# Up product's whole tiles in one 512-wide piece, turns reordered, and late forms of the down product queued behind streamed weights

## The chip, the cores and the metric

The kernel runs on one core of one Trainium2 chip. The metric is the device time of one execution in microseconds (us); less is better. Three runs of the kernel before gave 828.09, 829.57 and 830.15 us, so the median is 829.57 us.

## The reference, cut to what matters

One layer of an encoder trunk, on 512 positions (`SEQ`) of width 1024. The change touches only the second half, a gated MLP with a convolution of width 3 between the two products, and the norm that leads into it:

```python
x = x + _rmsnorm(merged @ w_out, g_post_mix)
h2 = _rmsnorm(x, g_pre_ffn)
x = x + _rmsnorm(_conv_gated_mlp(h2, w_up, conv_w, conv_b, w_down), g_post_ffn)
...
hid = h @ w_up                        # 1024 -> 2 * 2816
hid = conv(hid, width 3) + conv_b     # along the positions, each column by itself
a, b = jnp.split(hid, 2, axis=-1)
return (jax.nn.gelu(a) * b) @ w_down  # 2816 -> 1024
```

All is float32.

## The kernel before, in words

**Numbers as pairs.** Each float32 operand of a large product is split into a high part, rounded to TensorE's `float32r` format, and a low part, the rest (`split`, line 85: ScalarE copies the high part at line 80, VectorE subtracts at line 87, so most of VectorE's work has line 87). A product then takes three matmuls: high by high, high by low, low by high (`mm3`, lines 219 to 221). In a matmul one operand of 128 columns is loaded into the array (LDWEIGHTS, the engine PEld of the profile) and the other streams past it, 256 or 512 columns wide.

**The weights** come in 146 blocks of 128 x 1024 from one tensor `wall`, each by one DMA on SyncE's queue, into 4 raw buffers. They are split into 9 slots (`slot`, tag `w4`). `w_get` hands out the next block and lets the following ones be prepared ahead, as far as slots are free. A second pool, `blk`, holds 76 tiles of 128 x 512 for nearly everything else.

**Products of seven.** Many products are made in Strassen's manner, with seven smaller products in place of eight, from sums and differences of operands that ScalarE and VectorE (and GpSimd for some weights) prepare. In the up product these are `Pair`s (line 676); in the down product `products` (line 1062).

**From the mixing half to the MLP.** `dn_.finish(t, n)` ends the product with `w_out` for the 128 positions of tile `t` (0 to 3) and one half `n` of the columns (lines 830 to 832). `norms(t)` scales the result, adds the residual and makes the normed, scaled rows `xn` (line 882). `turn(t)` transposes them on TensorE (line 895) and, for each of four pieces, copies the high part `h2h` on ScalarE, copies the plain value `h2r` on ScalarE and makes the low part `h2l` on VectorE (line 901). Both `h2h` and `h2l` are kept in two groups, positions 0 to 255 (`T0`) and 256 to 511 (`T1`). The up product of the first four column tiles starts with their `T0` half (`early(e, 0)`, e from 0 to 3), while tiles 2 and 3 are still being normed; `turn(2)` stands after `early(0, 0)` and `turn(3)` after `early(3, 0)`. Then come the four `T1` halves.

**The up product** makes 44 tiles of 128 columns, two for each of 22 steps `i`. Steps 0, 1 (the early ones), 2, 3, 20 and 21 take both tiles whole: `up_block` runs eight slices `k` of the weights against `T0`, 24 matmuls, and then again against `T1`. Steps 4 to 19 go in eight couples: of the four tiles of a couple two are a `Pair` (seven products of 12 matmuls each, 256 wide) and two are whole; the second whole tile has part 3 of the Pair, two products, between its two halves. `tile_done` then does convolution (lines 971, 974, 978), gelu (985) and the product of the halves, `gp` (987).

**The down product** has 2 x 9 column tiles in the manner of seven and 4 whole ones, and goes over the 1024 output columns in two halves. In each half nine pairs `j` are taken one after the other; a pair is 42 matmuls on two weight units, `q` (loaded as it is, 128 x 768) and `t` (sums of four quarters, lines 185 to 190, 128 x 1024). After pairs 3 and 5 of the first half stand 48 matmuls for whole tiles (line 1079). `down_forms(j)` prepares the activation side of pair `j`: five steps on 128 x 256 and three on 128 x 512 on VectorE (lines 87, 1000 to 1003) and four copies on ScalarE. `two_parts` splits one whole tile. `EAGER = 7` of the nine forms are made during the up product: four at steps 7, 11, 13 and 17, three at steps 19, 20 and 21. The other two are made at pairs 1 and 3 of the down product, and one whole tile is split at each of pairs 0 to 3.

**What sets the order.** The program is traced in the order of the code, and a scheduler then orders each engine's instructions by priority and by its own idea of when inputs are there. Each engine runs its instructions strictly in that order. `tc.issue_after(ins)` forces the instructions of a block that run on `ins`'s engine to stand behind `ins` there.

## Time and profile before

| | us |
|---|---|
| median of three runs | 829.57 |
| the profiled execution, its own time | 826.92 |
| span of the profiled execution, first to last instruction | 825.1 |
| TensorE matmul (PE) busy | 814.5 |
| TensorE weight load (PEld) busy | 756.6 |
| VectorE (DVE) busy | 658.5 |
| ScalarE (ACT) busy | 429.7 |
| GpSimd (POOL) busy | 104.2 |

The stages around the change, read from the timeline of PE: the product with `w_out` ends at 471.6 us of the span; the `T0` halves of the early tiles and the last two turns follow until 485.6; the `T1` halves and the whole tiles of steps 2 and 3, then the couples; steps 20 and 21 end at 703.9; the first half of the down product runs to about 764 us, the second half to 808; the rest is the last norm and the output.

In a row of the timeline stand the start in us, the time it covers, the engine, the line, what is written and read, how many instructions the row merges, and in brackets the idle time before it with what ended it. Since matmuls overlap, the pace of PE is read from the starts of its matmuls and not from their durations: a row's duration of 0.28 us goes with a start every 0.11 us. The ends of matmuls are modelled, so a wait between two matmuls shows as a late start and only its last part as idle time.

### The profile page before, as it was taken

Reading aid. Unit: us, or ns where it says so; the run is one execution under the profiler, and the core shown is the slowest. Engines: PE = TensorE matmul, PEld = TensorE weight load, DVE = VectorE, ACT = ScalarE, POOL = GpSimd, SP = SyncE. Lnnn points to the kernel's source line nnn. Section 1 sums busy time; section 2 is a strip of 40 time slices with the busy share of each in tenths; the row PEclk is TensorE's granted clock in tenths of the full one; section 3 lists DMA queues with packets and bytes.
Section 4 is the critical chain, followed back from the end, with each engine's and each line's share of the span. In section 5 each row is a group of like instructions: output and inputs, shape, how many; then the busy total and the mean of one; then the engine's idle time right before and its main releaser. Section 6 shows DMA issues by size and latency. Waiting matters only on the chain. (4 is left out here: it accounts for less than half of the span.)

```text
span 825.1 us, 14353 instructions
## 1 busy us (share of the span) xinstructions
PE 814.5 (99%) x5728; PEld 756.6 (92%) x5728; DVE 658.5 (80%) x1076; ACT 429.7 (52%) x733; POOL 104.2 (13%) x108
## 2 busy tenths in 40 slices
PE   9999999999999999999999999999999999999995
PEld 7888888888999999999988899999999999999995
DVE  7489897878898687767765579679899899997956
ACT  6636445536665444444444556456566566644532
POOL 0010000103221111132221201111111100000002
PEclk9999999999999999999999999999999999999999
DMA  8733222213233333233459111333333341243334
GB/s 284 256 116 102 77 77 77 77 52 94 74 105 127 103 103 101 80 101 102 123 173 355 64 54 50 104 102 103 103 103 103 102 155 52 77 141 104 114 129 128
DMA packets 29252, 93.84 MB, mean 114 GB/s; under 512 B 3392, under 2 KB 4032, under 8 KB 29184
## 3 DMA queue, kind: packets, MB, share of 16 engines
q1 hardware_dynamic: 26784, 86.58, 32.5%
q0 software_dynamic: 1968, 6.03, 2.4%
q8 instruction: 45, 0.74, 0.4%
q10 hardware_dynamic: 432, 0.30, 0.1%
q14 instruction: 23, 0.19, 0.1%
HBM read 88.19 MB, written 4.72 MB: 113 GB/s over the span
## 5 line engine op out<-in xcount | busy, mean ns | idle before, releaser
L87 DVE TENSOR_TENSOR wl<-raw,wh 128x1024 fp32r<-128x1024 f32 (+1 forms) x93 | 109.6, 1187 | 49.2 <-PE ps L676 26.5
L80 ACT ACTIVATE wf<-raw 128x512 fp32r<-128x512 f32 x140 | 85.0, 626 | 102.4 <-PE ps L220 42.7
L87 DVE TENSOR_TENSOR wf<-raw,wf 128x512 fp32r<-128x512 f32 x140 | 110.1, 801 | 26.1 <-ACT wf L80 25.4
L220 PE MATMUL ps<-h2l,wh 128*128 128x256 f32 x448 | 123.7, 277 | 0.2 <-DVE h2l L901 0.2
L219 PE MATMUL ps<-h2h,wh 128*128 128x256 f32 x448 | 123.3, 277 | 0.0
L221 PE MATMUL ps<-h2h,wl 128*128 128x256 f32 x448 | 123.3, 276 | 0.0
L676 PE MATMUL ps<-sh,wf 128*128 128x256 f32 x640 | 119.1, 277 | 0.1
L80 ACT ACTIVATE wh<-raw 128x1024 fp32r<-128x1024 f32 (+2 forms) x95 | 93.0, 989 | 35.5 <-DMA raw<-wall 14.0
L676 PEld LDWEIGHTS ps<-sh,wf 128*128 128x128 f32 x640 | 100.7, 188 | 0.8 <-DVE c L704 0.3
L676 PE MATMUL ps<-sl,wf 128*128 128x256 f32 x320 | 88.5, 277 | 0.0
L220 PEld LDWEIGHTS ps<-h2l,wh 128*128 128x128 f32 x448 | 84.0, 188 | 0.7 <-DVE h2l L901 0.7
L219 PEld LDWEIGHTS ps<-h2h,wh 128*128 128x128 f32 x448 | 83.8, 188 | 0.3 <-ACT h2h L80 0.3
L221 PEld LDWEIGHTS ps<-h2h,wl 128*128 128x128 f32 x448 | 83.9, 188 | 0.0
L481 PE MATMUL ps<-wh,xh 128*128 128x512 f32 x192 | 75.0, 391 | 0.0
L482 PE MATMUL ps<-wl,xh 128*128 128x512 f32 x192 | 74.9, 390 | 0.0
L483 PE MATMUL ps<-wh,xl 128*128 128x512 f32 x192 | 74.8, 390 | 0.0
L168 POOL TENSOR_TENSOR raw<-raw,raw 128x512 f32<-128x512 f32 x20 | 34.9, 1743 | 241.0 <-DVE raw L166 217.0
L1062 PE MATMUL ps<-dh,fl 128*128 128x256 f32 x216 | 61.0, 282 | 0.0
L1062 PE MATMUL ps<-dl,fh 128*128 128x256 f32 x216 | 60.3, 279 | 0.5 <-DVE dl L87 0.5
L1062 PE MATMUL ps<-dh,fh 128*128 128x256 f32 x216 | 60.6, 280 | 0.0
L676 PEld LDWEIGHTS ps<-sl,wf 128*128 128x128 f32 x320 | 60.1, 188 | 0.5 <-issue 0.2
L676 PE MATMUL ps<-xh,wf 128*128 128x256 f32 x288 | 53.6, 278 | 0.0
(309 smaller groups left out, 2035.0 us busy)
## 6 DMA issues: line engine op xcount, KB each, us to landing
raw<-wall SPq DMA_DIRECT2D x145, 512.0 KB, 3.6
x<-x SPq DMA_DIRECT2D x22, 256.0 KB, 5.7
xT<-xT SPq DMA_DIRECT2D x8, 256.0 KB, 5.3
x<-x POOLq DMA_DIRECT2D x8, 256.0 KB, 2.4
xT<-xT POOLq DMA_DIRECT2D x4, 256.0 KB, 4.3
out<-zs SPq DMA_DIRECT2D x3, 256.0 KB, 3.4
cs<-cs SPq DMA_DIRECT2D x2, 256.0 KB, 4.0
gpm<-gpost POOLq DMA_DIRECT2D x2, 256.0 KB, 3.7
```

The costliest lines, as they stand in the source:

```text
L80: nc.scalar.activation(out=o, in_=i, func=AF.Copy)
L87: nc.vector.tensor_sub(lo, src, as32(hi))
L168: nc.gpsimd.tensor_tensor(out=w_raw["T2"], in0=w_raw["T1"], in1=w_raw["B22"], op=ALU.add)
L219: nc.tensor.matmul(o, ah, bh, start=start, stop=False)
L220: nc.tensor.matmul(o, ah, bl, start=False, stop=False)
L221: nc.tensor.matmul(o, al, bh, start=False, stop=stop)
L481: nc.tensor.matmul(acc[t], xh[k][:, c], wh[:, f], start=k == 0, stop=False)
L482: nc.tensor.matmul(acc[t], xh[k][:, c], wl[:, f], start=False, stop=False)
L483: nc.tensor.matmul(acc[t], xl[k][:, c], wh[:, f], start=False, stop=k == KD - 1)
L676: nc.tensor.matmul(o, w_[:, c], a_, start=first and k == n == 0, stop=k == 3 and n == 2, skip_group_check=True,)
L1062: nc.tensor.matmul(o, a_[:, c], w_[:, f], start=j == t == i == 0, stop=j == DP - 1 and i == 2 and n not in (M2, M3, M4), skip_group_check= ...
```

## The change

1. **Tiles.** `h2h` and `h2l` are now four tiles each that hold two slices `k` of all 512 positions, in a new pool `two` (8 tiles of 128 x 1024) which they share with the parts of the first input, `xh` and `xl`, and later with parts of the down product. In return `blk` shrinks from 76 to 60 tiles.
2. **Up product.** `up_block` multiplies each slice `k` against all 512 positions at once: 24 matmuls 512 wide instead of 48 that are 256 wide. Part 3 of a Pair now stands after the fourth of the eight slices. The early tiles stay in two halves. The weights of the whole tiles lose their shift within a slot.
3. **Turns.** `turn` makes high and low parts first and the four plain copies at its end. The scaled rows of tile 2 are made behind the low parts of `turn(1)` on VectorE. `turn(3)` moves into the middle of `early(3, 0)`.
4. **Down product.** `EAGER` falls to 5. Forms 5 to 8 and the four splits of whole tiles come after pairs 0 to 5, each block of them behind the low part of the next pair's `t` weights on VectorE. The parts of the forms 7 and 8 and of the last two whole tiles lie in `two`.

The core of the diff:

```diff
-NBLK = 76
+NBLK = 60
-EAGER = 7
+EAGER = 5
+WIDE = 7
+    def two(dt=F32R, n="two"):
+        return sb.tile([P, 2 * S], dt, tag="two", bufs=8, name=nm(n))
...
     def turn(t, zs):
...
             for i in range(2):
...
                 copy(hi, pf)
-                copy(raw, pf)
-                v.tensor_sub(lo, pf, as32(hi))
+                low = v.tensor_sub(lo, pf, as32(hi))
+                raws.append((raw, pf))
+        for raw, pf in raws:
+            copy(raw, pf)
+        return low
...
     def up_block(between=None):
-        w, o = w_get(), ps()
-        h2_block(w, o, T0)
-        if between:
-            between()
-        h2_block(w, o, T1)
+        (wh, wl), o = w_get(), ps()
+        for k in range(KD):
+            if between and k == KD // 2:
+                between()
+            c = slice(k * P, (k + 1) * P)
+            mm3(o, wh[:, c], wl[:, c], *h2(k, slice(0, S)), k == 0, k == KD - 1)
         return o
...
     for t in range(NT):
         acc = [dn_.finish(t, 0)]
         if t > 1:
-            turn(t - 2, zs[t - 2])
+            low = turn(t - 2, zs[t - 2])
+        if t == 3:
+            with tc.issue_after(low.ins):
+                zs[2] = scaled(*xq)
         acc.append(dn_.finish(t, 1))
-        zs[t] = norms(t, acc)
+        xq = norms(t, acc)
+        if t != 2:
+            zs[t] = scaled(*xq)
     early(0, 0)
     turn(2, zs[2])
     for e in range(1, EARLY):
-        early(e, 0)
-    turn(3, zs[3])
+        early(e, 0, (lambda: turn(3, zs[3])) if e == EARLY - 1 else None)
...
-    late = list(range(EAGER, DP))
+    later = (("w", 0), ("w", 1), ("f", 5), ("w", 2), ("f", 6), ("w", 3), ("f", 7), ("f", 8))
     for j in range(DP):
-        if j < WHOLE:
-            whole.append(two_parts(gp[2 * DP + j]))
-        if j % 2 and late:
-            down_forms(late.pop(0))
         products(m, j, steps if j == DP - 1 else {})
+        if j + 1 < DP:
+            with tc.issue_after(w_low["t", DOWN0 + j + 1]):
+                for kind, i in {0: later[:1], 1: later[1:3], 2: later[3:4], 3: later[4:6], 4: later[6:7], 5: later[7:]}.get(j, ()):
+                    if kind == "w":
+                        whole.append(two_parts(gp[2 * DP + i], i > 1))
+                    else:
+                        down_forms(i)
```

What this moves on the engines, at three places. Names carry a number of the tile; in `a<-b,c` the tile `a` is written from `b` and `c`. First TensorE, in the second whole tile of the last couple, where part 3 of the Pair (`wf`, `sh`, `h2h` as its operands, line 676 before and 682 after) comes in; `ps_7476` and `ps_7004` are the tile's accumulator. Before:

```order
L220 MATMUL ps_7476<-h2l_4394,wh_7360 128x256
L221 MATMUL ps_7476<-h2h_4386,wl_7361 128x256
L219 MATMUL ps_7476<-h2h_4386,wh_7360 128x256
L220 MATMUL ps_7476<-h2l_4394,wh_7360 128x256
L221 MATMUL ps_7476<-h2h_4386,wl_7361 128x256
L676 MATMUL ps_7326<-h2h_4389,wf_7204 128x256
L676 MATMUL ps_7326<-h2l_4397,wf_7204 128x256
```

And now:

```order
L225 MATMUL ps_7004<-h2h_4376,wl_6913 128x512
L223 MATMUL ps_7004<-h2h_4376,wh_6912 128x512
L224 MATMUL ps_7004<-h2l_4380,wh_6912 128x512
L225 MATMUL ps_7004<-h2h_4376,wl_6913 128x512
L682 MATMUL ps_6878<-h2h_4377,wf_6780 128x256
L682 MATMUL ps_6878<-h2l_4381,wf_6780 128x256
```

Part 3 comes in at the same share of the tile, but the tile's own matmuls are half as many and twice as wide, so that PE passes from 512 wide to 256 wide and back here; there are three such passages in each couple.

Second VectorE between `norms(2)` and `norms(3)`. `xn` are the scaled rows of tile 2, `h2l` the low parts of `turn(1)`, `z` and `x` the norm of the tile. Before:

```order
L873 TENSOR_TENSOR x_844_4735<-x_844_4735,z_4755 128x512
L846 SCALAR_TENSOR_TENSOR qs_4761<-q_4747 128x1
L882 SCALAR_TENSOR_TENSOR xn_4765<-x_843_4734,qr_4762,gpr_4379 128x512
L882 SCALAR_TENSOR_TENSOR xn_4767<-x_844_4735,qr_4762,gpr_4380 128x512
L901 TENSOR_TENSOR h2l_4391<-ps_4787,h2h_4383 128x2x128
L901 TENSOR_TENSOR h2l_4393<-ps_4798,h2h_4385 128x2x128
L901 TENSOR_TENSOR h2l_4392<-ps_4787,h2h_4384 128x2x128
L901 TENSOR_TENSOR h2l_4394<-ps_4798,h2h_4386 128x2x128
```

And now:

```order
L879 TENSOR_TENSOR x_828_4719<-x_828_4719,z_4739 128x512
L909 TENSOR_TENSOR h2l_4379<-ps_4763,h2h_4375 128x2x128
L909 TENSOR_TENSOR h2l_4380<-ps_4763,h2h_4376 128x2x128
L909 TENSOR_TENSOR h2l_4381<-ps_4772,h2h_4377 128x2x128
L909 TENSOR_TENSOR h2l_4382<-ps_4772,h2h_4378 128x2x128
L852 SCALAR_TENSOR_TENSOR qs_4785<-q_4731 128x1
L891 SCALAR_TENSOR_TENSOR xn_4789<-x_827_4718,qr_4786,gpr_4371 128x512
L891 SCALAR_TENSOR_TENSOR xn_4791<-x_828_4719,qr_4786,gpr_4372 128x512
```

The four low parts moved ahead of the two scaled rows and of the small sum `qs` that these wait for.

Third VectorE in the down product, up to the low part of the `t` weights of pair 3 (`dl` with 128x1024; `dl` with 128x768 is that of a `q`). `fa`, `fs`, `fl` and `gp` at 128x256 are steps of a form. Before:

```order
L87 TENSOR_TENSOR fl_7956<-gp_7571,fh_7955 128x512
L87 TENSOR_TENSOR fa_7959<-gp_7033,fa_7959 128x256
L1000 TENSOR_TENSOR fs_7962<-gp_7033,gp_7044 128x256
L185 TENSOR_TENSOR raw_8117<-raw_8063 128x512
L1001 TENSOR_TENSOR fs_7962<-fs_7962,gp_7033 128x256
L87 TENSOR_TENSOR fl_7968<-gp_7044,fh_7967 128x512
L1002 TENSOR_TENSOR gp_7033<-gp_7033 128x256
L87 TENSOR_TENSOR fl_7972<-fs_7962,fh_7971 128x512
L1003 TENSOR_TENSOR gp_7033<-gp_7044,fs_7962 128x256
L87 TENSOR_TENSOR dl_8008<-raw_8003,dh_8007 128x1024
```

And now:

```order
L91 TENSOR_TENSOR dl_7288<-raw_7283,dh_7287 128x1024
L194 TENSOR_TENSOR raw_7347<-raw_7347,raw_7323 128x256
L91 TENSOR_TENSOR fl_7380<-gp_7075,fh_7379 128x512
L91 TENSOR_TENSOR dl_7326<-raw_7323,dh_7325 128x768
L91 TENSOR_TENSOR fa_7383<-gp_6173,fa_7383 128x256
L1021 TENSOR_TENSOR fs_7386<-gp_6173,gp_6184 128x256
L1022 TENSOR_TENSOR fs_7386<-fs_7386,gp_6173 128x256
L91 TENSOR_TENSOR fl_7392<-gp_6184,fh_7391 128x512
L91 TENSOR_TENSOR dl_7352<-raw_7347,dh_7351 128x1024
```

Before, nearly the whole of form 7 stands ahead of the low part of pair 3's `t`, and forms 5 and 6 are already made by then (further up); now form 5 is the first that has been begun there, four steps of it stand ahead, and forms 6, 7 and 8 follow in the same way behind the weights of later pairs.

More of the change, by code (lines that the diff above doesn't have):

```diff
@@ L192, in w_down @@
         hi, lo = slot("dh", 16, w), slot("dl", 48, w)
-        split(hi, lo, raw)
+        w_low[form, i] = split(hi, lo, raw).ins
         return hi, lo
@@ L243, in load_x @@
         nc.sync.dma_start(t, xT[k])
-        h_, l_ = blk(F32R, "xh"), blk(F32R, "xl")
+        if k % 2 == 0:
+            xp2.append((two(n="xh"), two(n="xl")))
+        h_, l_ = (a[:, k % 2 * S : (k % 2 + 1) * S] for a in xp2[-1])
         nc.scalar.activation(out=h_, in_=t, func=AF.Copy, scale=col(PRE + k))
@@ L853, in tile_block @@
     gpm, gpf = bcast(gpost, "gpm"), bcast(gpre, "gpr")
-    h2h, h2l, h2r = ([[blk(dt, n) for _ in range(4)] for _ in range(2)]
-                     for dt, n in ((F32R, "h2h"), (F32R, "h2l"), (F32, "h2r")))
+    h2h, h2l = ([two(n=n).rearrange("p (i s) -> p i s", i=2) for _ in range(4)] for n in ("h2h", "h2l"))
+    h2r = [[blk(n="h2r") for _ in range(4)] for _ in range(2)]
     x1 = [[dp_.tile([P, S], F32, tag=f"x1_{t}{n}", name=f"x1_{t}{n}") for n in range(2)] for t in range(NT)]
@@ L877, in norms, with scaled @@
                 nc.gpsimd.dma_start(out[t, :, 0:S], xt[0])
+        return xt, q
+    def scaled(xt, q):
         sc, _ = row_scale(q)
@@ L896, in turn @@
             for i in range(2):
-                hi, lo, raw = (h[g][2 * n + i].rearrange(two, i=2)[:, :, c] for h in (h2h, h2l, h2r))
-                pf = p[:, 2 * i * P : 2 * (i + 1) * P].rearrange(two, i=2)
+                hi, lo = (h[2 * n + i][:, :, t * P : (t + 1) * P] for h in (h2h, h2l))
+                raw = h2r[g][2 * n + i].rearrange("p (i n) -> p i n", i=2)[:, :, c]
+                pf = p[:, 2 * i * P : 2 * (i + 1) * P].rearrange("p (i n) -> p i n", i=2)
                 copy(hi, pf)
-                copy(raw, pf)
-                v.tensor_sub(lo, pf, as32(hi))
+                low = v.tensor_sub(lo, pf, as32(hi))
[3 more added lines that the diff above has]
+        return low
     def h2(k, t):
-        f = slice((k % 2) * 256, (k % 2 + 1) * 256)
-        g = t.start // 256
-        return h2h[g][k // 2][:, f], h2l[g][k // 2][:, f]
+        return tuple(h[k // 2][:, k % 2, t] for h in (h2h, h2l))
     h2forms = {n: [None] * 4 for n in ("S1", "S2", "S3", "S4")}
@@ L987, in gated, with two_parts @@
         v.tensor_mul(gp[-1], ca, cb)
-    def two_parts(t):
-        h_, l_ = blk(F32R, "fh"), blk(F32R, "fl")
+    def two_parts(t, wide=False):
+        if wide:
+            w = two(n="fw")
+            h_, l_ = w[:, :S], w[:, S:]
+        else:
+            h_, l_ = blk(F32R, "fh"), blk(F32R, "fl")
         split(h_, l_, t)
```

25 lines of the change are left out of this document (14 added, 11 removed).

## The prediction, on record before the changed kernel was run

> **What bounds the kernel now.** I read the page first: its busy row and the chain that ended last.
>
> ```profile
> PE 814.5 (99%) x5728; PEld 756.6 (92%) x5728; DVE 658.5 (80%) x1076; ACT 429.7 (52%) x733; POOL 104.2 (13%) x108
> ```
>
> TensorE (PE) is busy for 99% of the span, so the kernel is bounded by the pace of its matmuls and by the few waits between them. Then I read busy times in stretches of 25 us (columns: PE, PEld, DVE, ACT, POOL busy with counts, granted clock, DMA share, GB/s).
>
> ```profile
> 425.00:450.00 25.00, 25.00 (x112) 20.71 (x111) 15.79 (x21) 13.17 (x22) 5.66 (x9) 1.00 0.79 290
> 500.00:525.00 25.00, 25.00 (x223) 25.00 (x222) 23.68 (x36) 14.68 (x24) 2.59 (x2) 1.00 0.26 86
> 700.00:725.00 25.00, 24.52 (x210) 24.31 (x209) 25.00 (x44) 15.89 (x25) 0.00 (x0) 1.00 0.26 85
> ```
>
> In the first stretch PE runs matmuls 512 wide, in the second matmuls 256 wide, twice as many. The clock is full in all. In the third, where the up product ends and the down product begins, VectorE (DVE) has no free time at all and PE makes 13 matmuls fewer than in the second. The wait list of PE has few rows here:
>
> ```profile
> PE ps L1062 <- DVE dl L87: 0.5, 1, 0.5
> PE ps L220 <- DVE h2l L901: 0.2, 1, 0.2
> ```
>
> These are idle times by modelled ends; the true size of a wait is read below from the starts in the timeline.
>
> **Change 1: 512 wide instead of 256.** First and last rows of two long undisturbed runs, 48 and 162 matmuls apart (16 and 54 times three):
>
> ```profile
> 426.31 0.39 PE L830 MATMUL ps<-wh,mh 128*128 128x512 f32 x1
> ...
> 437.19 0.39 PE L830 MATMUL ps<-wh,mh 128*128 128x512 f32 x1
> ```
>
> ```profile
> 499.74 0.28 PE L219 MATMUL ps<-h2h,wh 128*128 128x256 f32 x1
> ...
> 518.10 0.28 PE L219 MATMUL ps<-h2h,wh 128*128 128x256 f32 x1
> ```
>
> 10.88 / 48 = 0.2267 us at 512 wide and 18.36 / 162 = 0.1133 us at 256 wide. Twice the second is the first: a wide matmul takes as long as the two that it replaces, and the weight load that is saved was hidden. The change makes 576 wide matmuls (24 whole tiles of 24) from 1152 narrow ones; 576 x (0.2267 - 2 x 0.1133) = 0.0 us, with 0.2 us either way for the last digit. The Trainium skill ("TensorE: Matmul & The Clock Gate", section "Back-to-back issue gap") gives N / 2.4 + 2.5 ns between starts, so a fixed 2.5 ns per matmul, and by it, as an estimate, the 576 saved matmuls would give 1.4 us; the rows leave no room for it.
>
> But PE now changes width within the couples. That already happens earlier in the kernel, where a block of 24 wide matmuls stands between narrow ones:
>
> ```profile
> 305.16 0.40 PE L219 MATMUL ps<-gh,wh 128*128 128x512 f32 x1
> ...
> 310.62 0.28 PE L676 MATMUL ps<-sh,wf 128*128 128x256 f32 x1
> ...
> 311.20 0.39 PE L676 MATMUL ps<-sh,wf 128*128 128x256 f32 x2
> ```
>
> The block takes 5.46 us where 24 x 0.2267 are 5.44, and the next five, 310.62 to 311.20, take 0.58 where 5 x 0.1133 are 0.57: some 0.03 us a passage. There are three in each of 8 couples and one at steps 2 and 3: 25 x 0.03 = 0.8 us more, on PE and so on the path. Bounds: 0 and 1.0.
>
> **Change 2: the turns.** PE at the start of the first early tile, and at the return from `turn(3)`:
>
> ```profile
> 471.62 0.28 PE L219 MATMUL ps<-h2h,wh 128*128 128x256 f32 x1
> ...
> 473.42 0.28 PE L219 MATMUL ps<-h2h,wh 128*128 128x256 f32 x1
> ```
>
> ```profile
> 484.55 1.03 PE L895 MATMUL ps<-ident,xn 128*128 128x128 f32 x8
> 485.62 0.86 PE L219 MATMUL ps<-h2h,wh 128*128 128x256 f32 x5
> ...
> 486.70 0.28 PE L219 MATMUL ps<-h2h,wh 128*128 128x256 f32 x1
> ```
>
> Nine matmuls take 1.80 us instead of 1.02: 0.78 us lost to the low parts of `turn(1)`. At `turn(3)` the eight transposes should end near 485.43 (0.11 each), so the first matmul is 0.19 late, and the next eight, to 486.70, take 1.08 instead of 0.91: 0.36 lost. Both can go. What VectorE does ahead of `turn(1)`'s low parts:
>
> ```profile
> 470.12 1.41 DVE L882 SCALAR_TENSOR_TENSOR xn<-x,qr,gpr 128x512 f32<-128x512 f32 x2 [0.74 <-POOL qr L849]
> 471.46 0.74 DVE L901 TENSOR_TENSOR h2l<-ps,h2h 128x256 fp32r<-128x256 f32 x2
> 472.60 0.98 DVE L901 TENSOR_TENSOR h2l<-ps,h2h 128x256 fp32r<-128x256 f32 x2 [0.39 <-ACT h2r L80]
> ```
>
> The two `xn` (1.41) and 0.74 of waiting for GpSimd now come behind, so the first pair of low parts can start some 2 us sooner, and ScalarE no longer makes plain copies between the high parts. I expect all four by 471.0, ahead of 471.62. What is late next would be `xn` itself: about 1.6 us later than before, near 473.1, while `turn(2)` needs it after 24 matmuls of `early(0, 0)`, 471.62 + 2.72 = 474.34. It is covered by 1.2 us. The norm of tile 3 queues behind it on VectorE, but was itself late by ScalarE's copies, so it ends no later. At `turn(3)` the second half of `early(3, 0)`, 12 x 0.1133 = 1.36 us, now lies over the copies. Sum: -0.78 - 0.36 = -1.1 us; bounds -1.1 and 0.
>
> One thing goes with it. Between the two turns the same narrow matmuls run at a slower pace:
>
> ```profile
> 476.35 0.28 PE L219 MATMUL ps<-h2h,wh 128*128 128x256 f32 x1
> ...
> 484.20 0.28 PE L219 MATMUL ps<-h2h,wh 128*128 128x256 f32 x1
> ```
>
> 7.85 us for 66 (22 times three) is 0.1189 each, 0.0056 above the good pace, 0.37 us in all, and after the wait at 485 the good pace is back. With that wait gone the slow pace may last through the 96 matmuls of the `T1` halves (0.0056 x 96 = +0.54), or may not arise (-0.37). I take 0 and keep both.
>
> **Change 3: late forms.** The one longer wait of the down product, and VectorE ahead of it:
>
> ```profile
> 720.82 0.28 PE L1062 MATMUL ps<-dh,fh 128*128 128x256 f32 x1
> 721.58 0.39 PE L1062 MATMUL ps<-dl,fh 128*128 128x256 f32 x1 [0.48 <-DVE dl L87]
> 721.81 0.28 PE L1062 MATMUL ps<-dh,fl 128*128 128x256 f32 x1
> ```
>
> ```profile
> 709.47 0.42 DVE L87 TENSOR_TENSOR fa<-gp,fa 128x256 fp32r<-128x256 f32 x1
> ...
> 710.14 1.22 DVE L87 TENSOR_TENSOR dl<-raw,dh 128x1024 fp32r<-128x1024 f32 x1
> 711.27 0.42 DVE L1001 TENSOR_TENSOR fs<-fs,gp 128x256 f32<-128x256 f32 x1
> ...
> 713.48 0.95 DVE L87 TENSOR_TENSOR dl<-raw,dh 128x768 fp32r<-128x768 f32 x1
> 714.35 0.68 DVE L87 TENSOR_TENSOR fl<-gp,fh 128x512 fp32r<-128x512 f32 x1
> 714.95 0.42 DVE L189 TENSOR_TENSOR raw<-raw,raw 128x256 f32<-128x256 f32 x1
> ...
> 717.50 0.68 DVE L185 TENSOR_TENSOR raw<-raw 128x512 f32<-128x512 f32 x1
> 718.10 0.42 DVE L1001 TENSOR_TENSOR fs<-fs,gp 128x256 f32<-128x256 f32 x1
> ...
> 720.31 1.22 DVE L87 TENSOR_TENSOR dl<-raw,dh 128x1024 fp32r<-128x1024 f32 x1
> ```
>
> PE loses 0.99 us less two matmuls at the stage's 0.118, 0.75 us, to the low part that starts at 720.31. A form costs VectorE 714.95 - 709.47 less the two `dl` in between (1.13 and 0.87), 3.48 us. With two forms fewer ahead of it this low part can start about 7 us earlier, so this wait goes: -0.75.
>
> The price is in pairs 1 to 5, where VectorE must now make four forms between weights. By the starts above a pair's weights cost it 1.13 + 0.87 + 0.60 (L185) + 2 x 0.34 (L189, L190) = 3.3 us. PE takes, from the chain in order of time,
>
> ```profile
> 730.22 9.89 PE ps L1062 x84
> 740.11 5.65 PE ps L1079 x48
> ```
>
> 9.89 / 2 = 4.95 us for a pair, and 5.65 for each block of whole tiles, in which VectorE has 1.2 us of weights. A pair with a form is 3.3 + 3.5 - 4.95 = 1.8 us over; one without is 1.65 under, a whole block 4.4 under. The low part of `t` can start when the slots of two pairs back are free and ScalarE's copy is made, and is due 4.95 + 2.1 us after they are (a `t` comes in after 3 of 7 products): 7.05 less about 2.2 of work leaves 4.8 us. Forms stand after pairs 1, 3, 4 and 5, with whole blocks behind pairs 3 and 5, so VectorE is never more than about 3.6 us behind (two forms, after pairs 3 and 4, would be that even without the block). So it is covered, by about 1 us. DMAs, SyncE's and GpSimd's queues keep their order there.
>
> **A wait that stays.** In the sixth couple PE waits for a weight form behind VectorE's queue:
>
> ```profile
> 636.74 0.28 PE L676 MATMUL ps<-h2h,wf 128*128 128x256 f32 x1
> 637.09 0.38 PE L676 MATMUL ps<-sh,wf 128*128 128x256 f32 x1
> 637.31 0.28 PE L676 MATMUL ps<-sl,wf 128*128 128x256 f32 x1
> ```
>
> 0.57 less 0.23 is 0.34 us. The forms at steps 11 and 13, which fill VectorE there, are not moved: 0, bounds -0.34 and 0. The smaller `blk` I cost at nothing: the 16 tiles it gives up were those of `h2h` and `h2l`, or of `xh` and `xl` before them.
>
> **Sum.** 0.0 + 0.8 - 1.1 + 0 - 0.75 + 0 = -1.1 us against 826.92 us of the profiled execution (its span of 825.1 and 1.8 around it), so 825.8 there. The median of the runs is 829.57, 2.65 above that execution, by scatter alone (the three runs lie within 2.1 us); so 828.5 us. A measurement of this kernel can tell about 0.3% (2.5 us) from no change.
>
> **Rivals.** *A: all of it comes in.* Passages cost nothing, every wait named goes and so does the slow pace: 0.78 + 0.36 + 0.37 + 0.75 + 0.34 = 2.6 us, 827.0, just beyond 0.3%; for it stands that wide matmuls leave the weight loads more room, against it that every passage in the trace costs. With a saving per instruction on top it would be more, and against that stands that the 512-wide stretch, with 20.71 of 25 us of loads, has the same pace per column as the narrow one with 25.00. Chance 0.2. The Trainium skill ("Perfetto Trace Analysis", section "Identifying the Most-Contended Engine") judges TensorE by its weight-load busy time, and by that rule halving the loads should pay here; the two stretches disagree.
>
> *B: part is given back.* The slow pace lasts through the `T1` halves and one of the two waits at the turns stays: -1.1 + 0.54 + 0.36 = -0.2, 829.4. For it: the good pace came back before only behind a wait. Chance 0.25.
>
> *C: slower, by VectorE in the down product.* If the cover of 4.8 us is not there, because ScalarE's copies, which alternate with VectorE's steps within a form, hold up the weights that queue behind a form, PE waits for `t` after the two forms between the blocks: up to 2 x 1.8 = 3.6 us in place of the 0.75: -1.1 + 0.75 + 3.6 = +3.3, 832.8. It decides once VectorE is over 4.8 us behind. Against it stands the working above. Chance 0.1.
>
> That the deferral is not what it says is excluded: the order shows it.
>
> **Numbers.** The forecast has 0.45. Faster by over 0.3% is A, 0.2; slower is C, 0.1; within 0.3% the forecast and B, 0.7. With the scatter of a median, about 1 us, 8 in 10 lie from 826.0 (A's 827.0 and its scatter) to 830.6 (B and its scatter), with C left out.
>
> **What would show it.** Right: 512-wide rows 0.227 apart in the up product and the first five after a narrow one slower; no late start near 471.6, 485 and 720; 210 or more matmuls in every 25 us of the down product. Wrong: wide rows clearly under 0.22 apart, waits of PE for `dl` or `fl` in pairs 4 to 8, or the up product from the first wide tile to the down product longer by more than 1.5 us.

## The result, and the profile after

The changed kernel takes 826.33 us (median of nine runs, 825.53 to 827.91), the kernel before beside it 829.0 (nine runs, 827.54 to 830.15): a ratio of 0.9967, 95% interval 0.9955 to 0.9979. So it is 2.7 us faster, where 1.1 was forecast (828.5, range 826.0 to 830.6). The profiled execution of the changed kernel took 826.7 us, its span is 824.9: only 0.2 us less than the 826.92 and 825.1 of the profiled execution of before. That one lies below all nine timed runs shown beside it, so most of the gain isn't in these two traces. Both things need an explanation.

From the page after, the busy row, and from the wait list of PE its first row:

```profile
PE 813.9 (99%) x5152; PEld 734.1 (89%) x5152; DVE 657.8 (80%) x1076; ACT 430.6 (52%) x733; POOL 104.0 (13%) x108
```

```profile
PE ps L1083 <- DVE c L1115: 1.3, 1, 1.3
```

576 matmuls fewer, 22.5 us less of weight loading (PEld), and 0.6 us less of PE. The waits for `dl` and `h2l` are gone from the list; a new one, at the change of halves in the down product, is the largest.

**The turns.** The timeline of PE at the first early tile, where nine matmuls took 1.80 us before, and then the return from `turn(3)` and the slow pace behind it:

```profile
471.31 0.28 PE L223 MATMUL ps<-h2h,wh 128*128 128x256 f32 x1
...
472.34 0.28 PE L223 MATMUL ps<-h2h,wh 128*128 128x256 f32 x1
...
482.84 0.36 PE L223 MATMUL ps<-h2h,wh 128*128 128x256 f32 x1
483.04 0.28 PE L224 MATMUL ps<-h2l,wh 128*128 128x256 f32 x1
...
485.07 0.28 PE L223 MATMUL ps<-h2h,wh 128*128 128x256 f32 x1
...
495.41 0.28 PE L223 MATMUL ps<-h2h,wh 128*128 128x256 f32 x1
```

Nine matmuls now take 1.03 us. After `turn(3)` only one start is late, by 0.09. But the slow pace lasts: 10.34 us for 87 matmuls is 0.1189 each, through all `T1` halves.

**Wide and narrow.** The first matmul of the first couple and of the sixth, before and after:

```profile
518.44 0.28 PE L676 MATMUL ps<-h2h,wf 128*128 128x256 f32 x1
...
620.44 0.28 PE L676 MATMUL ps<-h2h,wf 128*128 128x256 f32 x1
```

```profile
517.58 0.28 PE L682 MATMUL ps<-h2h,wf 128*128 128x256 f32 x1
...
620.08 0.28 PE L682 MATMUL ps<-h2h,wf 128*128 128x256 f32 x1
```

Five couples take 102.00 us before and 102.50 after: 0.5 for 15 passages, 0.033 each. Of the 0.5, 0.39 lie on the wide matmuls and 0.11 on the narrow ones. The wide matmuls themselves save nothing.

**The sixth couple.** PE, where it lost 0.34 us before, and VectorE's step that reads the third bank of the Pair, after and before:

```profile
636.36 0.28 PE L682 MATMUL ps<-h2h,wf 128*128 128x256 f32 x1
636.47 0.28 PE L682 MATMUL ps<-sh,wf 128*128 128x256 f32 x1
```

```profile
634.34 0.42 DVE L710 TENSOR_TENSOR c<-ps,c 128x256 f32<-128x256 f32 x1
```

```profile
636.63 0.41 DVE L704 TENSOR_TENSOR c<-ps,c 128x256 f32<-128x256 f32 x1
```

The wait is gone. In the kernel before PE went on at 637.09, 0.05 after this step ended; it adds into the bank that the step reads. In the changed kernel the scheduler has the step ahead of two weight forms.

**The down product.** PE where the low part of pair 3's `t` was late, then at the change of halves, with VectorE there:

```profile
719.14 0.28 PE L1083 MATMUL ps<-dh,fh 128*128 128x256 f32 x1
...
722.18 0.28 PE L1083 MATMUL ps<-dh,fl 128*128 128x256 f32 x1
...
762.21 0.28 PE L1083 MATMUL ps<-dh,fl 128*128 128x256 f32 x1
763.78 0.39 PE L1083 MATMUL ps<-dh,fh 128*128 128x256 f32 x1 [1.29 <-DVE c L1115]
```

```profile
761.31 1.22 DVE L91 TENSOR_TENSOR dl<-raw,dh 128x1024 fp32r<-128x1024 f32 x1
762.44 0.68 DVE L1114 TENSOR_TENSOR yy<-ps,e 128x512 f32<-128x512 f32 x1
763.04 0.68 DVE L1115 TENSOR_TENSOR c<-ps,uu 128x512 f32<-128x512 f32 x1
```

The 26 matmuls from 719.14 take 3.04 us, 0.117 each, with no late start: the wait of 0.75 is gone. But at 762.21 PE loses 1.45 us (1.57 less one matmul), where the kernel before lost 0.15 at the same place: PE arrives 1.65 us earlier, VectorE only 0.35. It still has a low part of 1.22 us ahead of the two steps that free a bank.

Told as the lead of the changed kernel over before when each starts the same piece of work: -0.4 us at 7 us, +0.3 at 261 (the kernel before ran at the slow pace from 246 to 261 in that execution), +1.07 at 473, +1.37 at 486, +0.89 at 497, +0.30 at 634, +0.73 at 637, +0.62 at 719, +1.38 at 722, +1.65 at 762, +0.34 at 764.

### The profile page after: what moved, and what is told of

The parts are those of the page before. It is cut to its first block, busy times and chain, and to the rows that moved or that the text cites. A ratio compares the mean times of both kernels' runs of the same rounds, so it can differ in the third digit from the quotient of the medians.

```text
span 824.9 us, 13202 instructions
## 1 busy us (share of the span) xinstructions
PE 813.9 (99%) x5152; PEld 734.1 (89%) x5152; DVE 657.8 (80%) x1076; ACT 430.6 (52%) x733; POOL 104.0 (13%) x108
## 4 chain that ended last, share of the span: by engine, by line
PE 93%; DVE 3%; DMA 2%; issue 1%; POOL 1%; ACT 0%; POOLq 0%; DVEq 0%
PE ps L682 23%; PE ps L224 12%; PE ps L223 12%; PE ps L225 12%; PE ps L1083 8%; PE ps L488 5%; PE ps L487 5%; PE ps L489 5%; PE ps L836 2%; PE ps L837 2%; PE ps L838 2%; DMA raw<-wall 1%; PE ps L1100 1%; PE ps L761 1%; DVE dl L91 1%
## 5 line engine op out<-in xcount | busy, mean ns | idle before, releaser
L224 PE MATMUL ps<-h2l,wh 128*128 128x512 f32 (+1 forms) x256 | 93.1, 364 | 0.0
L223 PE MATMUL ps<-h2h,wh 128*128 128x512 f32 (+1 forms) x256 | 93.0, 363 | 0.0
L225 PE MATMUL ps<-h2h,wl 128*128 128x512 f32 (+1 forms) x256 | 92.5, 361 | 0.0
L225 PEld LDWEIGHTS ps<-h2h,wl 128*128 128x128 f32 x256 | 48.1, 188 | 7.7
L223 PEld LDWEIGHTS ps<-h2h,wh 128*128 128x128 f32 x256 | 48.1, 188 | 6.9
L224 PEld LDWEIGHTS ps<-h2l,wh 128*128 128x128 f32 x256 | 48.0, 188 | 6.6
L1083 PE MATMUL ps<-dh,fh 128*128 128x256 f32 x168 | 47.1, 280 | 1.3 <-DVE c L1115 1.3
L84 ACT ACTIVATE dh<-raw 128x768 fp32r<-128x768 f32 (+1 forms) x36 | 33.9, 948 | 25.6 <-PE ps L1083 19.5
L1083 PE MATMUL ps<-dh,fl 128*128 128x256 f32 x168 | 47.2, 281 | 0.0
```

Source lines behind the costliest of these rows:

```text
L84: nc.scalar.activation(out=o, in_=i, func=AF.Copy)
L223: nc.tensor.matmul(o, ah, bh, start=start, stop=False)
L224: nc.tensor.matmul(o, ah, bl, start=False, stop=False)
L225: nc.tensor.matmul(o, al, bh, start=False, stop=stop)
L1083: nc.tensor.matmul(o, a_[:, c], w_[:, f], start=j == t == i == 0, stop=j == DP - 1 and i == 2 and n not in (M2, M3, M4), skip_group_check= ...
```

## The experiments

Four theories are tested. Theory 1 (pace): PE has a good and a slow pace for narrow matmuls, 0.1134 and 0.118 to 0.119 us, and keeps the one it has until something ends it; the kernel before runs at the slow one for a part of the up product in most executions, and the changed kernel's whole tiles end it. Theory 2 (sum): the two profiled executions are typical, and the change is worth the 0.2 us between them. Theory 3 (clock): the granted clock differs. Theory S, which came later: the shift of the weights in their slots sets the pace. Each time stands beside runs of the kernel before on the same chip in the same hour. Between such groups the median of the kernel before itself moves by 2 us, so a ratio stands beside each time. A ratio has a weakness here, though: the times of the kernel before fall into two groups, as the next section shows, and where their shares differ the ratio moves with them.

### The two kernels again

No edit.

> The kernel before once more, unchanged, for a second profiled execution and the clock of every timed one. Its nine timed runs had a median of 829.0 us, its profiled execution took 826.92, less than any of them; the changed kernel has 826.33 and 826.7. Theory 1 (pace): in most executions of the kernel before a part of the narrow matmuls of the up product runs at the slow pace of 0.118 us in place of 0.1133, and the profiled one had little of it. Then this profile, if its time is 828 or more, shows 2 us more of slow pace between 487 and 704 us, at the same waits. Theory 2 (the sum): the two profiled executions are typical and only -0.2 us comes from the change; then times here come out near 827, and the 829.0 was the other chip. Theory 3 (clock): the granted clock is lower in the slow ones, by 0.002 for 2 us.

> The changed kernel once more, unchanged, on the same chip as the kernel before in the same hour, since the kernel before gave 829.0 in nine runs, but 827.3 in 29 and 828.2 in 12 others, from 825.6 to 830.3 each time. If the gain of the first comparison is real, 826.3 here and the kernel before 827.3 to 829; theory 1 (the kernel before falls into the slow pace in part of its executions, where the wide matmuls of the changed kernel end it) has a narrow scatter here, within 825.5 to 828, and a wide one before. Rival: the changed kernel scatters as much, and the two are within 0.1%.

> The kernel before a third time, for another profiled execution. Theory 1 (pace kept): if it takes 828 us or more, there is a stretch of slow pace in the up product behind 490 us (or in the Pairs before 470) that the executions of 826.92 and 827.36 don't have, worth 0.005 us for each matmul in it, and it ends at a wait of PE. If it takes under 828 there is none. Theory 3 (clock): no such stretch, and a lower granted clock.

The kernel before: 828.23 us (12 runs, 825.74 to 830.05) beside 827.29 (29 runs, 825.58 to 830.34) of itself. The changed kernel: 825.97 (8 runs, 825.38 to 826.81) beside 828.77, ratio 0.9969 (0.9958 to 0.9981), as in the first comparison. Of 84 runs of the kernel before, all those beside which another kernel was timed, 59 took 828.0 to 830.5 and 25 took 825.55 to 827.92; of the 17 of the changed kernel none took 828. The clock doesn't tell them apart: runs of 825.97 and of 829.81 had 0.996, of 825.7 and of 829.73 had 0.998. So theory 3 falls. Theory 2 falls too: the gain came again, and profiled executions of 826.92 and 827.36 are not typical of a kernel that takes 828 or more in two runs of three.

The third profiled execution of before took 828.21. PE in 25 us of the last couples (the count behind `x` is that of its matmuls), first in the execution of 826.92, then in this one:

```profile
650.00:675.00 25.00, 25.00 (x223) 25.00 (x222) 22.48 (x35) 15.01 (x25) 2.94 (x2) 1.00 0.43 129
```

```profile
650.00:675.00 25.00, 25.00 (x212) 25.00 (x211) 20.31 (x33) 14.63 (x25) 2.94 (x2) 1.00 0.40 137
```

11 matmuls of 223 fewer at a clock of 1.00, which is 4.9%, and of the 66 us from 637 to 703 that is 3.2 us. Matmul by matmul, this execution is 1.30 us ahead of the one of 826.92 when both start the same piece of work at 637 us, and 1.95 behind at 704. (The 1.30 come from elsewhere: 0.4 at the start, 0.7 from 246 to 261, 0.2 at the turns.) But not all of the 3.2 is kept. Where PE lost 0.75 us in the execution of 826.92 to the low part of pair 3's `t`, here no matmul is late:

```profile
722.76 0.28 PE L1062 MATMUL ps<-dh,fh 128*128 128x256 f32 x1
722.88 0.28 PE L1062 MATMUL ps<-dl,fh 128*128 128x256 f32 x1
```

PE comes 1.94 us later than there, and that low part has been ready since 722.48. So 0.75 us come back here and 0.14 at the change of halves, and the slow stretch costs 2.4 us net. Of the four traced executions of the kernel before, the one of the next section included, two had the wait at 720 and two the slow stretch, none both.

The slow stretch begins here, in the timeline of PE and of ScalarE of the same execution:

```profile
633.99 0.28 PE L221 MATMUL ps<-h2h,wl 128*128 128x256 f32 x1
634.10 0.31 PE L676 MATMUL ps<-h2h,wf 128*128 128x256 f32 x1
634.25 0.28 PE L676 MATMUL ps<-h2l,wf 128*128 128x256 f32 x1
634.38 0.40 PE L676 MATMUL ps<-h2h,wf 128*128 128x256 f32 x2
```

```profile
633.07 0.63 ACT L80 ACTIVATE wf<-raw 128x512 fp32r<-128x512 f32 x1 [1.84 <-DVE raw L166]
633.61 0.36 ACT L80 ACTIVATE c<-ps 128x256 f32<-128x256 f32 x1
```

The first matmul of part 3 starts 0.13 us after the end of ScalarE's copy (633.97), which reads the bank that this matmul writes, and from it to the second there are 0.15 us instead of 0.113. That copy stood behind a weight copy which waited 1.84 us for VectorE, busy with the form of step 13. From there the pace is slow. In the two profiled executions of 826.92 and 827.36 it was slow from the same place too, but good again 2 us later, behind the wait of 0.34; here that wait came too, and did not end it. The starts differ already ahead of it: in those two the first matmul of part 3 starts 0.113 us after the one before it, in this execution and the two slow ones below 0.117 or 0.118. Five executions are too few to say whether that decides. In the changed kernel the same copy stands ahead of the weight copy, and begins 2.5 us before part 3 needs the bank:

```profile
632.56 0.38 ACT L84 ACTIVATE c<-ps 128x256 f32<-128x256 f32 x1 [0.60 <-PE ps L682]
```

### The wait of the sixth couple taken away in the kernel before

```diff
...
+            free = v.tensor_sub(c1[:, T1], self.b[2][:, T0], c1[:, T1])
+            tc.add_manual_dep(low["T1", UP0 + 32], free.ins.name, ...)
```

> The kernel before with two neighbouring VectorE steps of the sixth couple exchanged and nothing else: the step that reads the third bank of the Pair (line 704), for which PE waits at 636.7, comes ahead of a weight form that GpSimd's work slows to 1.66 us. The changed kernel has the two in that order. In the profiled executions of the kernel before this wait cost 0.34 us where the good pace came back behind it (826.92, 827.36), and 0.34 and 2.8 us where the slow pace stayed up to 703 us (828.21). Theory 1 (pace kept): without the wait most executions keep the good pace, so the upper group of times (828.2 to 830.4) is nearly gone: median 826.0 to 826.8, at or within 0.5 us of the changed kernel, 1.5 to 2.5 us less than the kernel before beside it. Rival: the kernel before falls into the slow pace by chance at many places; then the median goes down by 0.34 only and the upper group stays.

In the diff, `low` holds the low parts of the weight forms: that of the next couple's `T1` is put behind line 704 on VectorE. 828.07 us (12 runs, 826.25 to 829.92) beside 829.44, ratio 0.9989 (0.9975 to 1.0004), not clear of no change; six of the twelve runs are at 828 or more, beside 12 of the 17 of the kernel before. Theory 1's form of the expectation fails: the upper group stays. That is what the rival said, but its reason, chance at many places, is not what the profiled execution (828.66) shows:

```profile
634.63 0.31 PE L677 MATMUL ps<-h2h,wf 128*128 128x256 f32 x1
634.78 0.28 PE L677 MATMUL ps<-h2l,wf 128*128 128x256 f32 x1
...
635.97 0.28 PE L677 MATMUL ps<-h2h,wf 128*128 128x256 f32 x1
636.08 0.28 PE L677 MATMUL ps<-sh,wf 128*128 128x256 f32 x1
```

```profile
650.00:675.00 25.00, 25.00 (x213) 25.00 (x212) 20.79 (x34) 14.45 (x24) 2.94 (x2) 1.00 0.41 131
```

The wait at 636 is gone (0.11 from 635.97 to 636.08), so PE did wait for line 704 there. The delay at the first matmul of part 3 is the same, and the slow pace begins with it. So the fall begins 1.4 us ahead of the wait that I took away. All five profiled executions of narrow kernels with the old order there (826.92, 827.36, 828.21, 828.64, 828.66) have this delay of 0.04 us at the same matmul, and the slow pace from it on. That it is the trigger is argued from that; taking it away alone was not tried.

### The whole tiles narrow again, with and without the shift

```diff
...
-            mm3(o, wh[:, c], wl[:, c], *h2(k, slice(0, S)), k == 0, k == KD - 1)
...
+        h2_block(w, o, T0)
+        if between:
+            between()
+        h2_block(w, o, T1)
```

> The changed kernel with the whole tiles of the up product narrow again (two halves of 24 matmuls, 256 wide, and part 3 between them); turns and late forms stay as changed. Theory 1 (pace): wide matmuls end the slow pace each time, so without them it is slower than the changed kernel by 1.5 to 2.5 us, at 828 to 829. Theory 2 (the sum): the passages between widths cost 0.4 to 0.8 us by the traces, so without them it is faster by that, at 825.5 to 826; the wait at 636 may come back with 0.34.

832.21 us beside 827.29, ratio 1.0047 (1.0031 to 1.0064), slower than either theory had it. Then with the weights of the whole tiles shifted in the slot as before:

```diff
-                (slot("wh", 48), slot("wl", 16)) if UP0 <= i < UP0 + EARLY else (slot("wh"), slot("wl"))
+                (slot("wh", 48), slot("wl", 16)) if i >= UP0 else (slot("wh"), slot("wl"))
```

> The changed kernel with the whole tiles narrow again, and now their weights shifted in the slot as before. Without the shift it took 832.2: its whole tiles ran at 0.120 us a matmul, its Pairs at 0.1134, where the kernel before has 0.1134 in both. Theory S (shift): the shift alone buys the 0.0066 us, so 880 x 0.0066 = 5.8 us less than 832.2, so 826.4, within 0.3 us of the changed kernel less the passages (0.4 to 0.8): 825.5 to 826.4. Theory 1 (pace): narrow matmuls keep a slow pace once they are in it, so it scatters as the kernel before does, 825.5 to 829, median 1 us above the changed kernel. If the shift is not the cause, 832 again.

835.13 beside 828.77, ratio 1.0076 (1.0062 to 1.009): theory S, that the shift alone buys the pace, is wrong. PE's count in two couples, in the kernel before, without the shift, and with it:

```profile
525.00:545.00 20.00, 20.00 (x179) 20.00 (x178) 14.08 (x24) 10.52 (x19) 3.41 (x2) 1.00 0.34 106
```

```profile
525.00:545.00 20.00, 20.00 (x174) 20.00 (x173) 12.20 (x21) 9.84 (x17) 3.42 (x2) 1.00 0.30 102
```

```profile
525.00:545.00 20.00, 20.00 (x171) 20.00 (x170) 13.10 (x19) 10.28 (x17) 3.00 (x2) 1.00 0.31 103
```

Without the shift the whole tiles run slowly, 27 matmuls in 3.24 us, 0.120 each, and the Pairs between them at the good pace, 48 matmuls in 5.44 us, 0.1133 each:

```profile
526.09 0.28 PE L225 MATMUL ps<-h2h,wl 128*128 128x256 f32 x1
...
529.33 0.28 PE L225 MATMUL ps<-h2h,wl 128*128 128x256 f32 x1
...
539.29 0.28 PE L682 MATMUL ps<-h2h,wf 128*128 128x256 f32 x1
...
544.73 0.28 PE L223 MATMUL ps<-h2h,wh 128*128 128x256 f32 x1
```

With the shift everything is slow from `turn(2)` to the end of the up product, 0.1189 each, the Pairs too. Whether it must be so is what the next run asks: the same narrow and shifted matmuls, but with the turns as before.

> The changed kernel with the whole tiles narrow and shifted and the turns as before: of the change only the late forms and the new tiles are left. With the new turns the same narrow, shifted matmuls took 835.1, because from the turns on all of them, whole tiles and Pairs, ran at the slow pace of 0.118 to 0.121 us up to 703. Theory 1 (pace kept): a shifted narrow stream keeps the pace it has, good or slow; with the old turns it leaves them at the good pace, so this runs at 0.1134 in the up product until it falls out of it by chance: 825.5 to 829.5 with a wide scatter, median near 827.5, and 7 to 9 us less than 835.1. Rival (layout): the new tiles of h2h and h2l, 1024 wide, make a narrow, shifted matmul slow whatever came before: 834 to 836.

828.64 (11 runs, 827.96 to 829.74) beside 829.33, ratio 0.9995: 6.5 us less than 835.13, for turns that wait longer. That fits theory 1, and the new tiles are not the cause: narrow, shifted matmuls ran from 487 to 635 us at the pace with which they came out of the turns. The range, 7 to 9 less, was missed, because ten of the eleven runs lie in the upper group and the other took 827.96; the profiled one is slow from 635 on.

### Wide, with the shift put back

The edit is the second one above, in the changed kernel.

> The changed kernel with the shift of the weights of the whole tiles put back, matmuls wide. Theory S: a matmul 512 wide leaves the weight load twice the time, so the shift changes nothing: within 0.3 us of the changed kernel. Rival: the passages from wide to narrow and back (0.4 to 0.8 us) come from the missing shift, and it is faster by that.

832.53 beside 828.77, ratio 1.0048 (1.0033 to 1.0062): 6.5 us slower than the changed kernel, where nothing or a gain was expected. PE in a couple and a half, in the changed kernel and in this one:

```profile
600.00:620.00 20.00, 20.00 (x130) 18.10 (x129) 19.35 (x31) 12.21 (x23) 2.94 (x2) 1.00 0.26 84
```

```profile
600.00:620.00 20.00, 20.00 (x127) 18.00 (x126) 18.67 (x31) 12.41 (x22) 2.94 (x2) 1.00 0.31 106
```

Three of 130 matmuls fewer in 20 us, and 6.1 us from the end of the `T1` halves to the end of the up product. With the shift the slow pace comes back with the first wide tile of the first couple, the Pairs behind it are slow too (0.1189), and nothing ends it. So it isn't the width that ends the slow pace. Four kernels with the turns as changed can be laid side by side: without the shift the Pairs run at 0.1133 to 0.1137 us whether the whole tiles are wide (825.97) or narrow (832.21); with it they run at 0.1189 whether wide (832.53) or narrow (835.13). The missing shift ends the slow pace, and the width makes the missing shift cheap: unshifted whole tiles take 0.120 a matmul when narrow, and when wide 0.228, which is 0.114 for each 256 columns. The Trainium skill ("SBUF — State Buffer", sections "SBUF: two separate sides" and "Who interferes with whom") has TensorE read its weights and its moving operand through two independent ports that wait for nobody; the changed kernel and this one differ only in where the weights lie in their slots, by 64 and 192 bytes, and in 6.5 us.

### The turns as before

```diff
                 copy(hi, pf)
+                copy(raw, pf)
...
-        early(e, 0, (lambda: turn(3, zs[3])) if e == EARLY - 1 else None)
+        early(e, 0)
+    turn(3, zs[3])
```

> The changed kernel with the turns as before (plain copies between high and low parts, the scaled rows of tile 2 in their old place, turn(3) after the early tiles). Both theories: the waits of 0.78 near 471.6 and 0.36 near 485 come back, and the slow pace of the late T1 halves, which the changed kernel has until 517 us (0.5 us), goes: slower by 0.6 us, 826.7 to 827.1. If the waits at the turns are larger in timed runs than in the profile, up to 2 us slower.

827.26 (12 runs, 826.43 to 829.37) beside 827.29, ratio 0.9997 (0.9984 to 1.0011). By the ratios, 0.9967 and 0.9969 for the changed kernel, the turns would be worth 2.5 us; by the times, 826.33 and 825.97, they are worth 0.9 to 1.3, little more than the 0.4 to 0.8 expected. The ratio probably says too much, since 15 of the 29 runs of the kernel before here lie in its lower group, and only 3 of the 14 beside the 825.97. The changed kernel was not run beside these 29, so it is not shown. In its profiled execution the two waits are back, and the `T1` halves run at the good pace, first the changed kernel and then this one:

```profile
487.00:495.00 8.00, 8.00 (x70) 8.00 (x69) 8.00 (x12) 6.89 (x9) 0.00 (x0) 1.00 0.35 118
```

```profile
487.00:495.00 8.00, 8.00 (x73) 8.00 (x72) 7.95 (x14) 6.10 (x10) 0.00 (x0) 1.00 0.29 104
```

The trace accounts for 0.3 us of the difference up to the end of the `T1` halves, 1.1 of waits less 0.7 of pace. The rest stays open. Four of the twelve runs took 828.27 or more, with the unshifted wide tiles in place, so either the slow stretch arises beside them too, or something else costs as much.

### The late forms as before

```diff
-EAGER = 5
-WIDE = 7
+EAGER = 7
+WIDE = 6
...
+        if j < WHOLE:
+            whole.append(two_parts(gp[2 * DP + j], j > 1))
+        if j % 2 and late:
+            down_forms(late.pop(0))
         products(m, j, steps if j == DP - 1 else {})
```

> The changed kernel with seven forms made early and the other two and the four splits placed as before (forms 6 and 7 instead of 7 and 8 lie in the new pool, for room). In the two traces the changed kernel gains 1.1 us by 762 us of the span and loses 1.3 in one wait for a VectorE step at the change of halves. Theory of the sum: the wait at 720 comes back with 0.75 and the one at 762 shrinks to 0.26, so the same time within 0.3 us. Rival: the wait at 762 is only in the profiled execution, and timed runs keep the gain; then slower by 1 us, 827.3.

829.3 (12 runs) beside 827.29, ratio 1.0017 (1.0003 to 1.003): 3.0 to 3.3 us above the changed kernel by the times, 4 by the ratios, where no change or 1 us was expected. The wait at 720 comes back, but nearly four times as long:

```profile
720.77 0.28 PE L1083 MATMUL ps<-dh,fl 128*128 128x256 f32 x1
723.00 0.73 PE L1083 MATMUL ps<-dh,fh 128*128 128x256 f32 x4 [1.96 <-ACT dh L84]
724.26 0.38 PE L1083 MATMUL ps<-dl,fh 128*128 128x256 f32 x1 [0.54 <-DVE dl L91]
```

PE loses some 2.9 us there, of which 1.4 come back at the change of halves; over the whole down product the trace has 2.0 us more than the changed kernel's. In this kernel the clock does tell the runs apart: the four at 0.997 took 827.71 to 828.57, the eight at 0.994 or 0.995 took 828.75 to 830.61. What of the difference goes with the clock was not looked into. It is not a clean undoing: form 6 lies in the new pool here, whose tiles are in use until the up product ends, so its steps pile up behind 704 us. It shows that in this layout the deferral is needed, not what it is worth against the kernel before.

### The wait at the change of halves

The low part moved behind the two steps that free the bank:

```diff
-        v.tensor_sub(c12, m[M5], uu)
+        c = v.tensor_sub(c12, m[M5], uu)
+        tc.add_manual_dep(w_low["t", DOWN0 + NF // 2 + 1], c.ins.name, ...)
```

> The changed kernel with one VectorE step moved at the change of halves: the low part of the t weights of the second half's second pair (1.2 us) goes behind the two steps that free the bank for which PE waits there. In the trace of the changed kernel PE waits 1.45 us at 762.2 for the last of those steps. Theory of the sum: the wait shrinks to 0.3 us, 1.1 us faster than the changed kernel, 825.2. Rival: the wait is only in the profiled execution, or the next pair then waits for the moved low part (needed 3.7 us later): no change or up to 1 us slower.

825.12 (5 runs, 824.23 to 825.53) beside 828.77, ratio 0.9955 (0.9941 to 0.9969); the changed kernel beside the same runs 825.97. So 0.85 us, with the wait at 0.48 (0.60 less one matmul):

```profile
761.43 0.28 PE L1083 MATMUL ps<-dh,fl 128*128 128x256 f32 x1
762.03 0.39 PE L1083 MATMUL ps<-dh,fh 128*128 128x256 f32 x1 [0.32 <-DVE c L1115]
```

```profile
760.69 0.69 DVE L1114 TENSOR_TENSOR yy<-ps,e 128x512 f32<-128x512 f32 x1
761.29 0.68 DVE L1115 TENSOR_TENSOR c<-ps,uu 128x512 f32<-128x512 f32 x1
761.89 1.22 DVE L91 TENSOR_TENSOR dl<-raw,dh 128x1024 fp32r<-128x1024 f32 x1
```

And with two banks of the second half swapped as well:

```diff
-    ... (M6, M6), (M7, M5), (M4, M7), (M8, M4) ...
+    ... (M6, M6), (M7, M7), (M4, M5), (M8, M4) ...
```

> The changed kernel with the low part of the t weights behind the two steps that free the bank, as in the run at 825.12, and the banks of M7 and M4 of the second half swapped, so that the first product that needs the late bank is one product (0.7 us) later. By the trace of the run with the moved step alone what is left of the wait (0.6 us or less) goes: 824.5 to 825.1. Rival: nothing is left there, then 825.1 as without the swap.

824.48 (5 runs, 824.08 to 825.26) beside 829.33, ratio 0.9945 (0.9932 to 0.9959), and the wait has left the list. It is the fastest of the study: 0.55% below the kernel before, where the changed kernel is 0.33% and 0.31% below it.

## Why the prediction was right, and where it wasn't

The sign was right and the time, 826.33, lies in the range, near its lower end at 826.0; the size, -1.1 for -2.7, was not, and that the time still lies in the range is owed to the width given to scatter. By the steps of the prediction:

- **Width, 0.0, and passages, +0.8.** Right: 0.033 us a passage, and 25 of them make 0.83. The 576 matmuls saved gave nothing. The estimate of 1.4 us that stood beside it, by the fixed time per matmul of the Trainium skill ("TensorE: Matmul & The Clock Gate", section "Back-to-back issue gap", where the formula is given for a single matmul by itself), is not borne out: five couples with 240 matmuls fewer (48 each) took 0.5 us longer.
- **The shift of the weights.** It stood in the list of what changes and had no term. With the shift left in, the wide tiles would have made the kernel 6.5 us slower. This is the step that was missed.
- **Turns, -0.78 and -0.36.** Right in the traces: the lead grows by 0.77 at the first and 0.30 at the second.
- **The slow pace between the turns, 0, bounds -0.37 and +0.54.** It lasted through the `T1` halves, and the lead falls by 0.48 there: rival B's mechanism, near its bound. I took the middle of two ends of which only one could come true.
- **Late forms, -0.75.** Right at 720 (0.76) against the execution of 826.92, and only against executions like it: those with the slow stretch up to 703 had no wait at 720 to lose. The cover between the weights held: no wait for `dl` or `fl` in pairs 4 to 8, so rival C's mechanism did not appear. But I stopped there and didn't ask what is late next: PE, 1.65 us ahead, ran into VectorE's bank steps at the change of halves and gave back 1.3. The 0.26 at 763.86 that the trace of before had there (0.15 and 0.11 on two matmuls) was the sign of it.
- **"A wait that stays", 0, bounds -0.34 and 0.** This failed, and by the account above it is most of the missing gain. PE waited there for line 704, not for a weight form, and the scheduler moved that step and ScalarE's copy ahead of the forms. The 0.34 went, and with the copy went the delay with which, in three of five traced executions with the old order, 66 us of slow pace begin: 3.2 us, 2.4 of them net. One profiled execution did not show it: it was one of those that recover.
- **The median 2.65 above the profiled execution "by scatter alone".** This was the same mistake seen from the other side. A profiled execution below every timed run shown beside it was a sign that the others lose time in something that it doesn't.

Rival A came nearest to the time, with 827.0, but by luck and not the way it came: passages cost, the slow pace behind the turns stayed, and behind the 0.34 stood 2.4.

Of the signs named in advance, the wide rows 0.227 apart, the slower ones behind a narrow one and the missing late starts near 471.6, 485 and 720 came. The 210 matmuls in every 25 us of the down product did not: from 750 to 775 us there are 202, by the wait at the change of halves.

What is shown: the slow stretch from 635 to 703 in profiled executions of 828.21, 828.64 and 828.66; its absence in those of 826.92 and 827.36 and in the changed kernel's; and that whole tiles without the shift end a slow stretch, that of the `T1` halves. What is argued: that the timed runs without a trace fall into their two groups by the same stretch, and that the delay of 0.04 us starts it. Whether the changed kernel is free of it by the order of the copy or by the missing shift is open. The sizes fit. The two groups of the kernel before have medians of 826.59 and 829.11, 2.5 us apart, where the stretch costs 2.4 net; and the changed kernel, 826.33 and 825.97, is 0.3 to 0.6 below the lower one, where the two traces differ by 0.2. So on this reading most of the gain of the change is that its executions stay out of the upper group.

## What to carry to other kernels

When the profiled execution is faster than the timed runs, the cost to look for is one that it doesn't show: take a second and a third profile before the terms are summed. Count matmuls per stretch and not only waits: 5% of pace over 66 us was worth 3.2 us here, more than any wait in the list, and no wait list names it. A loss ahead of a late input is partly given back, so two losses in a row are not to be added. A gain ahead of a stage boundary is worth only what the next engine can follow, so ask at each boundary which steps free the banks, and what stands ahead of them in their queue.

## What the runs showed of the hardware

- A stream of float32r matmuls 256 wide has two paces at full granted clock, 0.1134 and 0.118 to 0.119 us, and keeps the one it has over more than 500 matmuls. In five traced executions the slow one began at a delay of 0.04 us at one matmul; a wait of 0.34 us ended it in two of the four that had this wait.
- Where the weights lie in a slot of 4352 bytes decides too, in the kernels traced here. Narrow and unshifted, 0.120 in every whole tile, with the good pace behind it; narrow and shifted by 192 and 64 bytes, either pace; wide and unshifted, back to 0.2267 after five to ten matmuls of 0.231; wide and shifted, 0.233 on average from the first couple to the end of the up product. Why was not found.
- The down product ran at 0.117 to 0.118 in every traced execution. Whether another place of its weights would bring it to 0.1134 was not tried; by an estimate from its 948 matmuls and these paces that would be worth 3 to 4 us.
